# Retention's value blocks moved ahead of its queries and keys, two of them as one block of 1024 columns with four seven-product units

## The chip, the cores and the metric

The kernel runs on one core of a Trainium2 chip. Its engines have instruction queues of their own, which run in order and wait for each other by semaphores: TensorE (PE in the profile; PEld is its loading of weights), VectorE (DVE), ScalarE (ACT), GpSimd (POOL) and SyncE (SP), which here only issues the DMAs. The metric is the device time of one execution in microseconds: before the change 2271.42 us, the median of three runs (2270.95 to 2271.64).

## What is computed

A decoder layer for 256 tokens of width 2048 in float32: a half FFN, two token mixers side by side (retention and sliding-window attention), a second half FFN, and a gated input embedding, each followed by a layer norm. Of this the change touches the first projections of the mixers:

```python
rq, rk, rv, rg, aq, ak, av, gate_r, gate_a = jnp.split(h @ w_in[i], SPLIT_POINTS, axis=-1)
rq = rotary(rq.reshape(B, S, RET_HEADS, RET_DK), positions, RET_DK, RET_THETA)
rk = rotary(rk.reshape(B, S, RET_HEADS, RET_DK), positions, RET_DK, RET_THETA) * (RET_DK ** -0.5)
rv = rv.reshape(B, S, RET_HEADS, RET_DV)
ro = head_group_norm(retention_chunkwise(rq, rk, rv), ret_gn_g[i]).astype(h.dtype)
```

`rq` and `rk` have 1024 columns each, `rv` has 2048: four blocks of 512.

## The kernel before

**Numbers in two halves.** Every matrix product is made of three matmuls: each operand is split into a high half (a cast by ScalarE, L98, tiles `h...`) and a low half (a subtraction by VectorE, L99, tiles `l...`), and low x high, high x high and high x low are summed in a PSUM bank (L374, L375, L376; for queries and keys L325 and L333). A weight chunk is 512 KB, 128 x 1024 values. One of values, `w_rv`, holds two k-tiles of 128 rows for 512 columns; with two halves of 128 tokens it costs TensorE 2 x 2 x 3 = 12 matmuls of 512 columns, ScalarE one cast and VectorE one subtraction.

**Sevens.** Where two column blocks of 512 are made together, two chunks (one of each column block, the same two k-tiles) form a 2 x 2 problem: two k-tiles by two column blocks, against two token halves by two k-tiles. A *plain* pair, `P`, is two `Single` chunks and takes 24 matmuls. A `Seven`, `S`, does the same with seven products instead of eight, 21 matmuls, at the price of sums: VectorE makes four sums of weights of 512 columns (L170 to L173, tiles `u`, `v`) and four low halves instead of two (of the first chunk, of a quarter `b`, of `u` and of `v`): eight operations. The tokens need sums too, *forms* (`forms_of`, `whole`, `seven_forms`): for each group of four k-tiles one addition of 1024 columns (L457), four of 256 (L445 to L448), a cast and a low half. At the end `seven_common` folds the banks of the four products p1, p6, p7 and q5 (bank names ending in `s0` to `s3`) with one copy and four VectorE operations (L479 to L483), and four more add the plain banks (`a0`, `a1`, `b0`, `b1`). The third to the sixth product of a seven use forms. A block with sevens holds all eight PSUM banks.

**The order of the work.** The order is written out by hand (`manual_schedule`). A planner (`plan`, `fill`, `take`, `done`) loads chunks and prepares them in the order of the plan as far ahead as places allow (`slots_for_weights`: so many of 46 places in SBUF, each of 4 KB per partition). After each chunk `run_side` also runs a step of `lazy`: first of all `sums_ahead`, which prepares sevens of the second FFN ahead of time (two operations L238 and L239, two L242 and L243, low halves L248 and L250) and stores them to DRAM, and a rotary table for the attention.

**This stage.** After the first FFN, `norm.first` does the rest of the layer norm while TensorE makes the first block of values, `rv0`, as its tokens become ready. `values` then splits the block's two banks (tiles `rvh`, `rvl`). Then come eight groups of queries and keys (`rqk`, 16 matmuls of 512 and 16 of 256 columns per two chunks, each group followed by a rotation, L1064 to L1075), then blocks 1, 2 and 3 of values (`tokens_out`, 96 matmuls each), then the gates of retention, during which the heads' scores run as side jobs with the decay tables (`dec`, asked for by ScalarE's queue). Both stages have 14 places for weights. Later in the mixers, two gate blocks `ga0` and `ga1` are already blocks of 1024 columns with four sevens each (`GATE_UNITS`, `mixer_block`), with 22 places.

Of the kernel before, what the change touches and what calls it, by code (L numbers as in the profile page):

```python
# [8 lines left out]
F32 = mybir.dt.float32  # L9
# [46 lines left out]
def layer(ctx: ExitStack, tc: tile.TileContext, io):  # L56
# [13 lines left out]
    def banks(name):  # L70
        return [bank(name + str(j)) for j in range(2)]

    def slot(shape, dt, name):
        return slots.tile(shape, dt, tag="slot", name=name)
# [22 lines left out]
    def split(dst_hi, dst_lo, src, lo_engine=None):  # L97
        act.copy(dst_hi, src)  # L98
        (lo_engine or dve).tensor_tensor(dst_lo, src, dst_hi, ALU.subtract)  # L99
# [119 lines left out]
    def sums_ahead(items, wait, every):  # L219


        def pause():
            for _ in range(every):
                yield

        pairs = [[Chunk(k) for k in items[0]]]
        for _ in range(wait):
            yield
        for j, (key, _) in enumerate(items):
            a, b = pairs.pop()  # L230
            b11, b21, b12, b22 = a.of(a.raw, 0), a.of(a.raw, 1), b.of(b.raw, 0), b.of(b.raw, 1)
            u, v = (slot([P, 2, 512], F32, w + a.name) for w in "uv")
            t1, t3, t2, t4 = (x.rearrange("p (g n) -> p g n", g=2) for x in (u[:, 0], u[:, 1], v[:, 0], v[:, 1]))
            parts = [slot([P, 2, 512], F32R, w + a.name) for w in ("hu", "lu", "hv", "lv")]
            uh, ul, vh, vl = parts
            away = [dram.tile([P, 2, 512], F32, name=f"{w}{a.name}") for w in ("hud", "lud", "hvd", "lvd")]
            put_by_sums[key] = away
            dve.tensor_tensor(t1, b11, b12, ALU.add)  # L238
            dve.tensor_tensor(t3, b12, b22, ALU.add)  # L239
            yield from pause()  # L240
            act.copy(uh, u)
            dve.tensor_tensor(t2, b11, t3, ALU.add)  # L242
            dve.tensor_tensor(t4, t2, b21, ALU.add)  # L243
            yield from pause()
            act.copy(vh, v)
            if j + 1 < len(items):
                pairs.append([Chunk(k) for k in items[j + 1]])
            dve.tensor_tensor(ul, u, uh, ALU.subtract)  # L248
            yield from pause()
            dve.tensor_tensor(vl, v, vh, ALU.subtract)  # L250
            for e in range(2):
                sync.dma_start(away[e], parts[e].bitcast(F32))
            yield from pause()
            for e in range(2, 4):
                sync.dma_start(away[e], parts[e].bitcast(F32))
# [44 lines left out]
    def slots_for_weights(n, ahead=45, far=90):  # L300
        room.update(slots=n, ahead=ahead, far=far)
# [84 lines left out]
    def tokens_out(key, n_k, lhs, ps, n=512, before=None):  # L386

        nk = 1024 // n
        sums = [Sum(ps[t][:, :n], n_k) for t in range(2)]
        for c in range(n_k // nk):  # L390
            u = take(key + (c,))
            tokens_chunk(u.chunk, c * nk, lhs, sums, (0, 1), range(nk))
            done(u)
            run_side()
# [9 lines left out]
    def block(name, units, keys, lhs, forms, sums, fold, before=None):  # L404


        sevens = [p for kind, p in units if kind != "P"]
        if sevens:
            p1, p6, p7, q5 = (Sum(bank(f"{name}s{j}"), len(sevens)) for j in range(4))
        for j, (kind, p) in enumerate(units):  # L410
            if before is not None:
                before(j)
            if kind == "P":
                for n in range(2):
                    u = take(keys(n, p))
                    tokens_chunk(u.chunk, 2 * p, lhs, [sums[t][n] for t in range(2)], (0, 1))
                    done(u)
                    run_side()
                continue
            u = take(keys(0, p))  # L420
            a11, a12 = (half_of(lhs(2 * p + e), 0) for e in range(2))
            a22 = half_of(lhs(2 * p + 1), 1)
            f5, f6, f7, f3 = forms(p)
            q2, q3, q4 = sums[0][0], sums[0][1], sums[1][0]
            steps = [
                (p1, a11, u.b11), (q2, a12, u.b21), (q3, f3, u.b22), (q5, f5, u.t1),
                (p7, f7, u.t3), (p6, f6, u.t2), (q4, a22, u.t4),
            ]
            if p == sevens[-1]:
                steps = [steps[j] for j in (0, 3, 5, 4, 1, 2, 6)]  # L430
            for to, left, right in steps:
                to.add(left, right)
            done(u)
            run_side()
            if p == sevens[-1]:
                fold(p1.ap, p6.ap, p7.ap, q5.ap)
# [27 lines left out]
    def units_of(order, sevens, ahead=()):  # L464

        sevens, ahead = list(sevens), list(ahead)
        plain = [p for p in range(KD // 2) if p not in sevens + ahead]
        of = {"S": sevens, "D": ahead, "P": plain}
        return [(kind, of[kind].pop(0)) for kind in order]

    def block_sums(ps, units, n_k):

        s = sum(kind == "S" for kind, p in units)
        return [[Sum(ps[t][n], n_k - (2 * s if t and n else s)) for n in range(2)] for t in range(2)]
# [16 lines left out]
    def plan_tokens(key, n_k, nk=2):  # L491
        for c in range(n_k // nk):
            plan.append(Single(key + (c,)))
# [585 lines left out]

    GATE_UNITS = units_of("PPSSPSSP", (0, 1, 2, 3))  # L1080
    RET_UNITS = units_of("PPPSPSPP", (0, 1))
    gate_keys = lambda b: lambda n, p: ("w_in_f2", 29 + 4 * b + 2 * n, p)
    ret_keys = lambda b: lambda n, p: ("w_ret2", 4 * b + 2 * n, p)

    def plan_mixers():
        plan_tokens(("w_rv", 0), KD)
        for grp in range(8):
            plan_features([("w_in_f", grp)], KD)
        for blk in range(1, 4):
            plan_tokens(("w_rv", blk), KD)  # L1090
        for grp in range(8, 16, 2):
            plan_tokens(("w_in_f2", grp), KD)
        plan_tokens(("w_av",), KD, nk=4)
        for grp in (20, 16, 17, 18, 19):
            plan_features([("w_in_f", grp)], KD)
        for grp in range(21, 29, 2):
            plan_tokens(("w_in_f2", grp), KD)
        for b in range(2):
            block_units(GATE_UNITS, gate_keys(b))
        for j in range(0, 8, 2):  # L1100
            plan_tokens(("w_att2", j), KD // 2)
        for b in range(2):
            block_units(RET_UNITS, ret_keys(b))
        for blk in range(4):
            plan_tokens(("w_mix", blk), KD)
# [7 lines left out]
    def mixers(ht, norm, residual, keepers, away):  # L1113
        cos_r, sin_r = trig["r"]
        rhs = lambda k: (ht[:, k, :S], ht[:, k, S:])
        both_halves = lambda k: ht[:, k, :]
        rq = [slot([P, 4, S], F32, f"rq{j}") for j in range(2)]
        rk = [slot([P, 4, S], F32, f"rk{j}") for j in range(2)]

        def rotated(grp, ps):  # L1120
            who = (rq, rk)[grp // 4][grp % 4 // 2]
            rotate(ps, f"rr{grp}", who[:, grp % 2 * 2 : grp % 2 * 2 + 2, :], cos_r, sin_r, SH_R)

        rv = []

        def values(blk, ps):
            hi, lo = (slot([P, 2, 512], F32R, f"rv{w}{blk}") for w in "hl")
            for t in range(2):
                split(hi[:, t], lo[:, t], ps[t])
            rv.append((hi, lo))  # L1130

        ps = banks("rv0")
# [7 lines left out]
            tokens_chunk(u.chunk, 2 * c, rhs, [sums[t][0] for t in range(2)], (0, 1))  # L1140
            done(u)
        values(0, ps)
        slots_for_weights(14)
        ahead = [(gu_keys("f2", j)(0, p), gu_keys("f2", j)(1, p)) for j in AHEAD for p in AHEAD[j]]
        lazy.append(sums_ahead(ahead[:2], 3, 2))
        lazy.append(rotary_table("a"))
        lazy.append(sums_ahead(ahead[2:5], 2, 2))
        lazy.append(sums_ahead(ahead[5:8], 2, 3))
        for grp in range(8):
            ps = banks(f"rqk{grp}")  # L1150
            features_out([(("w_in_f", grp), ps)], KD, both_halves)
            rotated(grp, ps)
        grp = 8
        decay = [slot([P, 2, 384], F32, f"dec{j}") for j in range(4)]
        for j in range(4):
            act.dma_start(decay[j], io["decay"][:, 2 * j : 2 * j + 2, :])
        for blk in range(1, 4):
            ps = banks(f"rv{blk}")
            tokens_out(("w_rv", blk), KD, rhs, ps)
            values(blk, ps)  # L1160

        ret_t = [None] * HR
        gate_v = [None] * HR
        keep = {}
# [223 lines left out]
        for grp in (18, 19):  # L1388
            attention_features(grp)

        made = {}
        forms = lambda p: made[p // 2](p % 2)
        slots_for_weights(18)
        sig = []
        for j in range(4):
# [8 lines left out]
            for t in range(2):  # L1404
                act.copy(sig[-1][:, t], ps[t])
        assert not side

        def mixer_block(name, units, keys, lhs):

            ps = [banks(name + w) for w in "ab"]  # L1410
            got = []
            block(name, units, keys, lhs, forms, block_sums(ps, units, KD), lambda *a: got.extend(seven_common(*a)))
            for n in range(2):
                for t in range(2):
                    dve.tensor_tensor(got[n][:, t], got[n][:, t], ps[t][n], ALU.add)
            return got

        slots_for_weights(22)
        for b in range(2):
# [375 lines left out]
```

## Time and profile before

| what | value |
|---|---|
| median of three runs | 2271.42 us |
| span of the profiled execution | 2269.2 us |
| TensorE's granted clock, mean | 0.999 |
| DMA | 515.72 MB, mean 227 GB/s |
| casts and low halves of the values' chunks (`hw_rv`, `lw_rv`) | 32 each, 1.05 and 1.22 us |
| last matmul of block 0 of values, first of the queries | 732.5 us, 732.7 us |
| blocks 1 to 3 of values | 822 to 887 us |

The profile is one execution, taken by the hardware profiler; times inside it count from its first instruction. Matmuls overlap, so their listed lengths (390 ns for 512 columns) are longer than the distance from one to the next. A row of the timeline gives start, length, engine, line, operation, tiles out and in with their shapes, a count, and the idle time of the engine before it with what ended it.

### The profile page before, as it was taken

Reading aid. Unit: us, or ns where it says so; the run is one execution under the profiler, and the core shown is the slowest. Engines: PE = TensorE matmul, PEld = TensorE weight load, DVE = VectorE, ACT = ScalarE, POOL = GpSimd, SP = SyncE. Lnnn points to the kernel's source line nnn. Section 1 sums busy time; section 2 is a strip of 40 time slices with the busy share of each in tenths; the row PEclk is TensorE's granted clock in tenths of the full one; section 3 lists DMA queues with packets and bytes.
Section 4 is the critical chain, followed back from the end, with each engine's and each line's share of the span. In section 5 each row is a group of like instructions: output and inputs, shape, how many; then the busy total and the mean of one; then the engine's idle time right before and its main releaser. Section 6 shows DMA issues by size and latency. Waiting matters only on the chain.

```text
span 2269.2 us, 29180 instructions
## 1 busy us (share of the span) xinstructions
PE 2262.1 (100%) x10497; PEld 1880.1 (83%) x10497; DVE 1996.8 (88%) x2586; ACT 1224.6 (54%) x1493; POOL 2.3 (0%) x9
## 2 busy tenths in 40 slices
PE   9999999999999999999999999999999999999998
PEld 8888888888888888888778888888888888888887
DVE  7999999999989887888789788689999999889887
ACT  6555555556555444445566554455555565555543
POOL 0000000000000000000000000000000000000000
PEclk9999999999999999999999999999999999999999
DMA  8666665665587878765446668787867766555872
GB/s 301 206 202 195 197 212 177 205 205 187 211 287 258 293 284 295 255 227 190 145 154 219 194 203 294 278 287 241 299 242 250 257 197 218 197 189 210 290 268 75
DMA packets 211130, 515.72 MB, mean 227 GB/s; under 512 B 16413, under 2 KB 20893, under 8 KB 210985
## 3 DMA queue, kind: packets, MB, share of 16 engines
q1 hardware_dynamic: 209000, 511.28, 66.4%
q10 hardware_dynamic: 1984, 2.58, 0.4%
q8 instruction: 82, 1.34, 0.2%
q14 instruction: 64, 0.52, 0.1%
HBM read 484.43 MB, written 29.36 MB: 226 GB/s over the span
## 4 chain that ended last, share of the span: by engine, by line
PE 99%; DVE 0%; ACT 0%; issue 0%; ACTq 0%; POOL 0%; POOLq 0%
PE f1g L376 3%; PE f1g L374 3%; PE f1g L375 3%; PE f2g L376 3%; PE f2g L374 3%; PE f2g L375 3%; PE rqk L325 3%; PE f1u L376 2%; PE f1u L374 2%; PE f1u L375 2%; PE f2u L374 2%; PE f2u L376 2%; PE f2u L375 2%; PE aqk L325 2%; PE f2d L374 2%; PE f1d L375 2%
## 5 line engine op out<-in xcount | busy, mean ns | idle before, releaser
L99 DVE TENSOR_TENSOR lf_gu<-rf_gu,hf_gu 128x1024 fp32r<-128x1024 f32 (+1 forms) x274 | 323.3, 1211 | 13.1 <-ACT hf_gu L98 12.2
L98 ACT CAST hf_gu<-rf_gu 128x1024 fp32r<-128x1024 f32 (+1 forms) x274 | 274.1, 1043 | 29.9 <-DMA rf_gu<-in_f_gu 29.6
L99 DVE TENSOR_TENSOR lf_down<-rf_down,hf_down 128x1024 fp32r<-128x1024 f32 x150 | 178.8, 1220 | 17.4 <-ACT hf_down L98 15.3
L99 DVE TENSOR_TENSOR lw_in_f<-rw_in_f,hw_in_f 128x1024 fp32r<-128x1024 f32 x140 | 167.5, 1219 | 24.9 <-ACT hw_in_f L98 24.7
L98 ACT CAST hf_down<-rf_down 128x1024 fp32r<-128x1024 f32 x150 | 151.8, 1050 | 48.8 <-DMA rf_down<-in_f_down 22.3
L98 ACT CAST huf_gu<-uf_gu 128x1024 fp32r<-128x1024 f32 x70 | 73.8, 1054 | 146.6 <-DVE uf_gu L171 135.1
L98 ACT CAST hw_in_f<-rw_in_f 128x1024 fp32r<-128x1024 f32 x140 | 140.3, 1050 | 3.0 <-PE rv L375 1.4
L374 PE MATMUL f1g<-hf_gu,xt 128*128 128x512 f32 x247 | 96.5, 391 | 0.0
L376 PE MATMUL f1g<-lf_gu,xt 128*128 128x512 f32 x247 | 96.4, 390 | 0.0
L375 PE MATMUL f1g<-hf_gu,xt 128*128 128x512 f32 x247 | 96.1, 389 | 0.0
L98 ACT CAST hvf_gu<-vf_gu 128x1024 fp32r<-128x1024 f32 x70 | 73.8, 1054 | 29.9 <-DVE vf_gu L173 29.2
L971 ACT ACTIVATE eve<-eve 128x1024 f32<-128x1024 f32 x20 | 21.2, 1062 | 126.1 <-DVE eve L970 126.1
L99 DVE TENSOR_TENSOR luf_gu<-uf_gu,huf_gu 128x1024 fp32r<-128x1024 f32 x70 | 85.3, 1219 | 0.0
L99 DVE TENSOR_TENSOR lvf_gu<-vf_gu,hvf_gu 128x1024 fp32r<-128x1024 f32 x70 | 85.3, 1218 | 0.0
L374 PE MATMUL f2g<-hf_gu,ht 128*128 128x512 f32 x217 | 84.6, 390 | 0.0
L376 PE MATMUL f2g<-lf_gu,ht 128*128 128x512 f32 x217 | 84.5, 390 | 0.0
L375 PE MATMUL f2g<-hf_gu,ht 128*128 128x512 f32 x217 | 84.4, 389 | 0.0
L374 PE MATMUL f1u<-hf_gu,xt 128*128 128x512 f32 x212 | 83.4, 393 | 0.0
L376 PE MATMUL f1u<-lf_gu,xt 128*128 128x512 f32 x212 | 82.5, 389 | 0.0
L375 PE MATMUL f1u<-hf_gu,xt 128*128 128x512 f32 x212 | 82.5, 389 | 0.0
L374 PE MATMUL f2u<-hf_gu,ht 128*128 128x512 f32 x172 | 68.2, 397 | 0.0
L376 PE MATMUL f2u<-lf_gu,ht 128*128 128x512 f32 x172 | 66.9, 389 | 0.0
(1465 smaller groups left out, 6558.1 us busy)
## 6 DMA issues: line engine op xcount, KB each, us to landing
rf_gu<-in_f_gu SPq DMA_DIRECT2D x360, 512.0 KB
rf_down<-in_f_down SPq DMA_DIRECT2D x176, 512.0 KB
rw_in_f<-in_w_in_f SPq DMA_DIRECT2D x148, 512.0 KB
rw_rv<-in_w_rv SPq DMA_DIRECT2D x32, 512.0 KB
rw_ret<-in_w_ret SPq DMA_DIRECT2D x32, 512.0 KB
rw_mix<-in_w_mix SPq DMA_DIRECT2D x32, 512.0 KB
rw_pg<-in_w_pg SPq DMA_DIRECT2D x32, 512.0 KB
rw_att<-in_w_att SPq DMA_DIRECT2D x16, 512.0 KB
```

What stands on the lines that cost most here:

```text
L98: act.copy(dst_hi, src)
L99: (lo_engine or dve).tensor_tensor(dst_lo, src, dst_hi, ALU.subtract)
L325: pe.matmul(ps[f], hi[:, kk, f * P : (f + 1) * P], rhs(k), start=k == 0, stop=k == n_k - 1,)
L374: pe.matmul(o, al, bh, start=first, stop=False)
L375: pe.matmul(o, ah, bh, start=False, stop=False)
L376: pe.matmul(o, ah, bl, start=False, stop=self.left == 0)
L971: act.activation(g, g, AF.Silu)
```

## The change

It does four things. The plan and the code put all values ahead of the queries and keys. Blocks 1 and 2 are made together as one block of 1024 columns by `mixer_block` (moved up, unchanged), with the units plain 4, seven 0, plain 5, seven 1, plain 6, seven 2, plain 7, seven 3; its token forms for two groups are made right after block 0, and `values` splits each folded result of 1024 columns at once. These blocks run with the 24 places that `norm.first` is followed by, and 14 places are set only before block 3. The tiles for queries and keys (four places) are taken only after block 3.

```diff
+    VALUE_UNITS = units_of("PSPSPSPS", (0, 1, 2, 3))
+    value_keys = lambda n, p: ("w_rv", 1 + n, p)
...
         plan_tokens(("w_rv", 0), KD)
+        block_units(VALUE_UNITS, value_keys)
+        plan_tokens(("w_rv", 3), KD)
         for grp in range(8):
             plan_features([("w_in_f", grp)], KD)
-        for blk in range(1, 4):
-            plan_tokens(("w_rv", blk), KD)
...
-        rq = [slot([P, 4, S], F32, f"rq{j}") for j in range(2)]
-        rk = [slot([P, 4, S], F32, f"rk{j}") for j in range(2)]
+        rq, rk = [None] * 2, [None] * 2
...
         def values(blk, ps):
             hi, lo = (slot([P, 2, 512], F32R, f"rv{w}{blk}") for w in "hl")
-            for t in range(2):
-                split(hi[:, t], lo[:, t], ps[t])
+            if isinstance(ps, list):
+                for t in range(2):
+                    split(hi[:, t], lo[:, t], ps[t])
+            else:
+                split(hi, lo, ps)
             rv.append((hi, lo))
...
         values(0, ps)
-        slots_for_weights(14)
+        for g in range(2):
+            made[g] = forms_of([ht[:, 4 * g : 4 * g + 4, :]], f"rvf{g}")
...
         lazy.append(sums_ahead(ahead[5:8], 2, 3))
+        for n, v in enumerate(mixer_block("rvs", VALUE_UNITS, value_keys, rhs)):
+            values(1 + n, v)
+        made.clear()
+        slots_for_weights(14)
+        ps = banks("rv3")
+        tokens_out(("w_rv", 3), KD, rhs, ps)
+        values(3, ps)
+        rq[:] = [slot([P, 4, S], F32, f"rq{j}") for j in range(2)]
+        rk[:] = [slot([P, 4, S], F32, f"rk{j}") for j in range(2)]
         for grp in range(8):
             ps = banks(f"rqk{grp}")
             features_out([(("w_in_f", grp), ps)], KD, both_halves)
...
             act.dma_start(decay[j], io["decay"][:, 2 * j : 2 * j + 2, :])
-        for blk in range(1, 4):
-            ps = banks(f"rv{blk}")
-            tokens_out(("w_rv", blk), KD, rhs, ps)
-            values(blk, ps)
```

More of the change, by code (lines that the diff above doesn't have):

```diff
@@ L1124, in mixers, with mixer_block @@
         rv = []
+        made = {}
+        forms = lambda p: made[p // 2](p % 2)
+        def mixer_block(name, units, keys, lhs):
+            ps = [banks(name + w) for w in "ab"]
+            got = []
+            block(name, units, keys, lhs, forms, block_sums(ps, units, KD), lambda *a: got.extend(seven_common(*a)))
+            for n in range(2):
+                for t in range(2):
+                    dve.tensor_tensor(got[n][:, t], got[n][:, t], ps[t][n], ALU.add)
+            return got
         def values(blk, ps):
             hi, lo = (slot([P, 2, 512], F32R, f"rv{w}{blk}") for w in "hl")
-            for t in range(2):
-                split(hi[:, t], lo[:, t], ps[t])
+            if isinstance(ps, list):
+                for t in range(2):
+                    split(hi[:, t], lo[:, t], ps[t])
+            else:
+                split(hi, lo, ps)
             rv.append((hi, lo))
@@ L1389, in mixers @@
             attention_features(grp)
-        made = {}
-        forms = lambda p: made[p // 2](p % 2)
         slots_for_weights(18)
@@ L1406, in mixers @@
         assert not side
[L1408 to L1416, printed above, removed]
         slots_for_weights(22)
```

## The prediction

> **What bounds the kernel now.** I read first the page's busy times, then TensorE's own waits.
>
> ```profile
> span 2269.2 us, 29180 instructions
> PE 2262.1 (100%) x10497; PEld 1880.1 (83%) x10497; DVE 1996.8 (88%) x2586; ACT 1224.6 (54%) x1493; POOL 2.3 (0%) x9
> ...
> PE warm L1674 <- POOL ident masks.py:199: 1.4, 1, 1.4
> PE pln L1568 <- DVE plnst L1566: 0.2, 1, 0.2
> PE plnt L1559 <- DVE plnm L1554: 0.2, 1, 0.2
> ```
>
> TensorE waits 1.8 us in 2269, so a matmul fewer is a matmul's time saved, and nothing else can be gained. VectorE is the second engine. Three stretches of the windows view show where it has room; the columns are the stretch, its length, then busy time of PE, PEld, DVE, ACT and POOL, TensorE's granted clock, DMA share and GB/s.
>
> ```profile
> 730.00:742.00 12.00, 12.00 (x66) 10.37 (x65) 9.98 (x11) 7.09 (x9) 0.00 (x0) 1.00 1.02 399
> 844.00:866.00 22.00, 22.00 (x99) 18.22 (x98) 15.65 (x17) 11.12 (x13) 0.00 (x0) 1.00 0.90 302
> 1200.00:1240.00 40.00, 40.00 (x178) 33.14 (x177) 39.42 (x48) 22.01 (x24) 0.00 (x0) 1.00 0.61 199
> ```
>
> The second is a plain block of values, with VectorE idle 6.3 of 22 us. The third is a gate block with four sevens: VectorE is busy 39.4 of 40 us, and TensorE holds only because the weights for the block were prepared during an easier stage before it. The change puts such a block right behind the norm (first row), where no easier stage lies ahead. So I follow VectorE's queue there by hand.
>
> **The gain.** Matmuls of 512 columns follow each other at one pace: 21 of them from the first row to the second.
>
> ```profile
> 727.98 0.23 PE rv L374
> ...
> 732.74 1.36 PE rqk L325 x6
> ```
>
> (732.74 - 727.98) / 21 = 0.2267 us. Two plain pairs of chunks cost 24 matmuls, a seven 21; four sevens save 12 x 0.2267 = 2.72 us. The order in which the built program issues its matmuls has 12 fewer, and no other kind is added.
>
> **What VectorE gets to do, and when.** These rows of its timeline give each price as the distance from one start to a later one, so that overlap is not counted twice. The columns are start, length, line, operation, tiles, count, and idle time before with its releaser.
>
> ```profile
> 728.41 6.89 DVE L99 TENSOR_TENSOR lw_in_f<-rw_in_f,hw_in_f 128x1024 fp32r<-128x1024 f32 x6
> 735.22 1.28 DVE L99 TENSOR_TENSOR rvl<-rv,rvh 128x512 fp32r<-128x512 f32 x2
> 736.42 2.35 DVE L99 TENSOR_TENSOR lw_in_f<-rw_in_f,hw_in_f 128x1024 fp32r<-128x1024 f32 x2
> ...
> 744.11 0.76 DVE L1065 TENSOR_TENSOR rr0v<-rqk,rr0lo 128x256 f32<-128x256 f32 x2 [4.13 <-ACT rr0lo L1064]
> ...
> 747.63 2.35 DVE L99 TENSOR_TENSOR lw_in_f<-rw_in_f,hw_in_f 128x1024 fp32r<-128x1024 f32 x2
> ...
> 828.09 0.69 DVE L238 TENSOR_TENSOR uf_gu<-rf_gu,rf_gu 128x512 f32<-128x512 f32 x1
> ...
> 829.30 2.35 DVE L99 TENSOR_TENSOR lw_rv<-rw_rv,hw_rv 128x1024 fp32r<-128x1024 f32 x2
> 831.57 0.69 DVE L242 TENSOR_TENSOR vf_gu<-rf_gu,uf_gu 128x512 f32<-128x512 f32 x1
> ...
> 832.90 2.35 DVE L99 TENSOR_TENSOR lw_rv<-rw_rv,hw_rv 128x1024 fp32r<-128x1024 f32 x2
> 835.17 1.22 DVE L248 TENSOR_TENSOR luf_gu<-uf_gu,huf_gu 128x1024 fp32r<-128x1024 f32 x1
> ...
> 1142.32 1.22 DVE L457 TENSOR_TENSOR gaf1w<-ht 128x1024 f32<-128x1024 f32 x1
> ...
> 1146.29 1.23 DVE L99 TENSOR_TENSOR gaf1l<-sums,gaf1h 128x1024 fp32r<-128x1024 f32 x1 [1.17 <-ACT gaf1h L98]
> 1147.44 1.22 DVE L99 TENSOR_TENSOR lw_in_f<-rw_in_f,hw_in_f 128x1024 fp32r<-128x1024 f32 x1
> ...
> 1169.47 0.69 DVE L170 TENSOR_TENSOR uw_in_f<-rw_in_f,rw_in_f 128x512 f32<-128x512 f32 x1
> ...
> 1176.14 0.68 DVE L170 TENSOR_TENSOR uw_in_f<-rw_in_f,rw_in_f 128x512 f32<-128x512 f32 x1
> 1203.20 0.69 DVE L480 TENSOR_TENSOR evw<-eve,ga0s 128x512 f32<-128x512 f32 x1
> ```
>
> A chunk's low half costs 6.81 / 6 = 1.14 us; block 0's two low halves 1.20; a seven's eight operations 1176.14 - 1169.47 = 6.67; one set of forms of the tokens 1147.44 - 1142.32 = 5.12, with 1.17 us of standing still for ScalarE in it; the first two sums prepared ahead for the second FFN 1.21, the next two 1.33, their low half 1.14; the first fold operation (L480) 0.69.
>
> Before, VectorE had eight chunks' low halves to make from 728.41 and then stood idle 4.13 us. In the changed program its queue from 728.41 on runs, in the order in which it is issued (my sums): two low halves of the plain pair 4, to 730.7; seven 0, 737.4; pair 5, 739.6; block 0's rvl, 740.8; forms 0, **746.0**; forms 1, 751.1; seven 1, 757.7; half of pair 6, two sums ahead, the other half, 761.2; seven 2, 767.9; two sums ahead, pair 7, one low half ahead, 772.7; seven 3, 779.3; four low halves of block 3's chunks with one low half ahead among them, 785.0; two sums ahead, 786.2; L480, **786.9**. That is 58.5 us of queue without a pause.
>
> **TensorE beside it.** It leaves block 0 at 732.74 as before.
> 1. Pair 4 takes 24 matmuls, to 738.2; the first two products of seven 0 need no forms, 6 more, to 739.5. The third multiplies the low half of form 0, ready at 746.0: it stands **6.5 us** (A). Seven 0 and pair 5 go on to 754.9.
> 2. Sevens 1 and 2 and pairs 6 and 7 just hold: seven 1's first low half is there at 751.1 + 6.67 - 0.60 - 2 x 1.14 = 754.9 (three low halves of it follow) and is needed by its third matmul at 755.3. Seven 3 does not: TensorE is there at 775.4; the low halves that its first three products need come at 776.5, 778.2 and 779.3, each later than the matmul before them allows, **some 2 us** (B).
> 3. Block 3's second bank is the one that product p6 leaves, and L480 reads that. TensorE has the rest of seven 3 and three matmuls into the first bank done near 783 and waits until 786.9, **some 4 us** (C).
>
> A shorter way to the same sum, which needs none of the middle: without a wait the 180 matmuls of the block and three of block 3 end at 732.74 + 183 x 0.2267 = 774.2. L480 ends at 786.9. Loss 12.7, gain 2.72: **10.0 us net**.
>
> After C, TensorE reaches chunk 4 of block 3 45 matmuls later, at 797.1; VectorE needs seven fold operations and block 1 and 2's rvl (7 x 0.65 + 2 x 1.14) and that chunk's low half, 794.9. From there VectorE leads again, with four chunks in hand at the queries; the groups of queries load it as they did.
>
> **TensorE's clock.** A wait of this length is nowhere inside the old kernel; only its ends show one.
>
> ```profile
> 2262.95 0.96 PE L1568 MATMUL pln<-lnrow,plnst 66*128 66x512 f32 x3 [0.21 <-DVE plnst L1566]
> ...
> 2262.00:2263.00 1.00, 0.79 (x4) 0.36 (x4) 0.86 (x3) 0.26 (x1) 0.00 (x0) 1.00 0.00 0
> ...
> 2264.00:2265.00 1.00, 0.00 (x0) 0.00 (x0) 0.59 (x1) 0.75 (x2) 0.00 (x0) 1.00 0.59 204
> 2265.00:2266.00 1.00, 0.00 (x0) 0.00 (x0) 0.00 (x0) 0.00 (x0) 0.00 (x0) 0.72 0.92 339
> 2266.00:2267.00 1.00, 0.00 (x0) 0.00 (x0) 0.00 (x0) 0.00 (x0) 0.00 (x0) 0.50 1.02 385
> ...
> L1674 PE MATMUL warm<-ident x19: 421/421/473, 1.4 to 5.3; 128*128 128x128 f32 x19
> ...
> L623 PE MATMUL lnps<-ident,f1y x32: 270/272/275, 701.6 to 724.3; 128*128 128x128 f32 x32
> ```
>
> The granted clock falls to a half about 1.5 us after the last matmul ends (2263.9), and the transposes of the start, which come from rest, take 421 ns against 272 for the same form later, for the whole 3.9 us from 1.4 to 5.3. If a wait does this here, some 3.9 us run at half pace: 1.95 us lost. After A it costs nothing more, because B and C end with VectorE's queue and swallow it. After C nothing follows that would: between 0 and 2.0. I take 1.3, nearer to the upper end, since C is 4 us long and the row falls after 1.5, but TensorE was already idle a fifth of the time before that (second row).
>
> [...]
>
> **Sum.** The profiled execution's span is 2269.2; the runs' median is 2271.42, 2.2 more, which lies around the span. 2271.4 + 10.0 + 1.3 = **2282.7 us**.
>
> **What is costed at nothing.** Weight loads: a pair of chunks fetched for seven 1 takes the places in the queue where two chunks for queries stood, and those were split at 736.42 without a DMA wait; seven 1 needs them at 751. The decay tables are now asked for right behind the queries and used in the first gate chunks.
>
> ```profile
> 822.16 0.33 ACTq L1156 DMA_DIRECT2D dec<-in_decay  x1
> ...
> 825.49 1.31 SPq L112 DMA_DIRECT2D rw_rv<-in_w_rv  x2
> ...
> SPq L112 <- DMA dec<-in_decay: 10.3, 3, 9.2
> ```
>
> The weight queue was released by the first table's landing at 825.5, 3.3 us after its issue; VectorE wants it after the last group's rotation (747.63 - 744.11 = 3.5) and one low half, 4.6 us after. Queued behind that wait are the low halves from the gates' sixth chunk on, needed 5 x 12 x 0.2267 = 13.6 us after the gates begin, and the scores of head 0, which TensorE wants after the third chunk, 8.2 us. A table that lands more than some 2 us late would cost; the price is 0 to 3 us.
>
> **Rivals.**
> - Not slower (4%): VectorE has the forms ready by 739.5, TensorE never waits, all 2.7 us stay: 2268.7. The gate block speaks for it, where the same work did not hold TensorE; against it, there the second set of forms was ready at 1147.4, some 15 us before the block began (its fold stands at 1203.2, 180 x 0.2267 = 40.8 after its start), and here both stand behind 12.4 us of queue. It decides at one point, whether forms 0 end before 739.5.
> - Forms alone (15%): A is paid, the rest is made up because sums ahead and block 3's halves get out of the way or the bank comes free sooner: 6.5 - 2.7 + 0 to 2 for the clock, 2275.2 to 2277.2.
> - More waits (11%): the decay tables or chunks fetched late add up to 3 us, or the clock stays low longer: 2285 to 2288.
> - Forecast (70%): 2281.4 to 2283.4.
>
> That the edit does not do what it says is out: 12 matmuls are gone from the program.
>
> **The numbers.** What this kernel can tell from no change is about 0.2%, 4.5 us: 2266.9 to 2276.0. All of the first rival and about two thirds of the second fall within; faster by more would need a gain which no row offers. Faster 0.02, same 0.14, slower 0.84. Range 2275 to 2287.
>
> **What would show it.** Right: 128x512 rv matmuls 12 fewer; TensorE idle 6 to 7 us with VectorE's low half of the forms as releaser; a second wait of about 4 us at block 3's second bank, released by L480; granted clock below 1 near both; TensorE's first query matmul near 809, gates some 10 us later than before. Wrong: no wait at the forms (first rival), no second wait (second rival), or a wait on the decay tables.

## The result and the profile after

| | before | after |
|---|---|---|
| median of the runs, side by side | 2271.53 us (2270.95 to 2271.95) | 2284.05 us (2283.23 to 2284.63) |
| span of the profiled execution | 2269.2 us | 2282.8 us |
| TensorE's granted clock, mean | 0.999 | 0.996 |

The ratio is 1.0055, 95% interval 1.0043 to 1.0067: the changed kernel is 0.55% slower. The gain is there all the same. The head of the page and its busy times (the last number in each part is the count of instructions) show 10485 matmuls where there were 10497:

```profile
span 2282.8 us, 29225 instructions
...
PE 2265.0 (99%) x10485; PEld 1881.8 (82%) x10485; DVE 2025.6 (89%) x2628; ACT 1233.5 (54%) x1502; POOL 2.3 (0%) x9
```

TensorE's waits (total, times, longest) now begin with two lines that were not there before, ahead of the one of the kernel's start:

```profile
PE rvsa L374 <- DVE rvf0l L99: 6.5, 1, 6.5
PE rv L374 <- DVE evw L480: 3.3, 1, 3.3
PE warm L1683 <- POOL ident masks.py:199: 1.4, 1, 1.4
```

The first is the wait for the forms (A in the prediction), the second the one for block 3's second bank (C). There is none at the last seven's low halves (B) and none on the decay tables. VectorE's timeline shows what TensorE waited for:

```profile
740.98 1.22 DVE L457 TENSOR_TENSOR rvf0w<-ht 128x1024 f32<-128x1024 f32 x1
...
744.90 1.23 DVE L99 TENSOR_TENSOR rvf0l<-sums,rvf0h 128x1024 fp32r<-128x1024 f32 x1 [1.11 <-ACT rvf0h L98]
...
779.52 1.22 DVE L99 TENSOR_TENSOR lw_rv<-rw_rv,hw_rv 128x1024 fp32r<-128x1024 f32 x1
780.65 1.22 DVE L250 TENSOR_TENSOR lvf_gu<-vf_gu,hvf_gu 128x1024 fp32r<-128x1024 f32 x1
781.79 3.49 DVE L99 TENSOR_TENSOR lw_rv<-rw_rv,hw_rv 128x1024 fp32r<-128x1024 f32 x3
785.19 0.69 DVE L238 TENSOR_TENSOR uf_gu<-rf_gu,rf_gu 128x512 f32<-128x512 f32 x1
785.79 0.69 DVE L239 TENSOR_TENSOR uf_gu<-rf_gu 128x512 f32<-128x512 f32 x1
786.39 0.68 DVE L480 TENSOR_TENSOR evw<-eve,rvss 128x512 f32<-128x512 f32 x1
```

The forms end at 744.90 + 1.23 = 746.13. The last seven's last low half is done by 779.52; then four low halves of block 3's chunks (the first of them is the row at 779.52) and three operations for the second FFN stand ahead of L480, which ends at 787.07. TensorE's timeline around both waits:

```profile
739.31 0.39 PE L376 MATMUL rvsa<-lw_rv,ht 128*128 128x512 f32 x1
746.18 0.80 PE L374 MATMUL rvsa<-bw_rv,rvf0l 128*128 128x512 f32 x1 [6.48 <-DVE rvf0l L99]
...
752.37 0.39 PE L374 MATMUL rvsa<-hw_rv,ht 128*128 128x512 f32 x1
...
783.42 0.39 PE L376 MATMUL rv<-lw_rv,ht 128*128 128x512 f32 x1
787.13 0.79 PE L374 MATMUL rv<-hw_rv,ht 128*128 128x512 f32 x1 [3.32 <-DVE evw L480]
...
793.32 0.40 PE L374 MATMUL rv<-hw_rv,ht 128*128 128x512 f32 x1
```

From 746.18 to 752.37 and from 787.13 to 793.32 lie 15 matmuls each: 6.19 us where 15 x 0.2267 = 3.40 are due. So each wait is followed by 2.79 us lost, nearly all of it at half clock: the first matmul takes 0.6 us, the twelve after it some 0.43 each, and the last two are back at nearly the full pace. The windows view has the clock in its third number from the end:

```profile
741.00:742.00 1.00, 0.00 (x0) 0.00 (x0) 1.00 (x2) 0.00 (x0) 0.00 (x0) 0.83 0.83 188
751.00:752.00 1.00, 1.00 (x4) 0.77 (x3) 1.00 (x3) 0.46 (x1) 0.00 (x0) 0.55 0.00 0
...
786.00:787.00 1.00, 0.00 (x0) 0.00 (x0) 1.00 (x2) 0.00 (x0) 0.00 (x0) 0.52 1.05 315
792.00:793.00 1.00, 1.00 (x4) 0.80 (x3) 1.00 (x2) 1.00 (x2) 0.00 (x0) 0.57 0.67 274
```

The account of the stage: 6.64 (739.31 to 746.18, less one matmul) + 2.79 + 3.48 (783.42 to 787.13, less one matmul) + 2.79 - 2.72 saved = 12.98 us. The first row of the retention gates, before and then after, says the same (the two numbers in us are the first and the last start in what is shown):

```profile
L374 PE MATMUL rg<-hw_in_f,ht x56: 389/389/478, 887.2 to 929.2; 128*128 128x512 f32 x56
```

```profile
L374 PE MATMUL rg<-hw_in_f,ht x39: 388/390/475, 900.4 to 929.8; 128*128 128x512 f32 x39
```

They start 13.2 us later, and the span is 13.6 longer: nothing comes back later, and next to nothing is added. (The profiled execution is the slowest of its four, at 2284.63 us; the medians lie 12.5 apart.)

### The profile page after: what moved, and what is told of

It is laid out like the page before. It is cut to its first block, busy times and chain, and to the rows that moved or that the text cites. A ratio compares the mean times of both kernels' runs of the same rounds, so it can differ in the third digit from the quotient of the medians.

```text
span 2282.8 us, 29225 instructions
## 1 busy us (share of the span) xinstructions
PE 2265.0 (99%) x10485; PEld 1881.8 (82%) x10485; DVE 2025.6 (89%) x2628; ACT 1233.5 (54%) x1502; POOL 2.3 (0%) x9
## 4 chain that ended last, share of the span: by engine, by line
PE 97%; DVE 1%; DMA 1%; ACT 0%; issue 0%; ACTq 0%; SPq 0%; DVEq 0%
PE f1g L374 3%; PE f1g L376 3%; PE f1g L375 3%; PE f2g L376 3%; PE f2g L375 3%; PE f2g L374 3%; PE rqk L325 3%; PE f1u L374 2%; PE f1u L375 2%; PE f1u L376 2%; PE f2u L375 2%; PE f2u L376 2%; PE f2u L374 2%; PE aqk L325 2%; PE f2d L374 2%; PE f1d L376 2%
## 5 line engine op out<-in xcount | busy, mean ns | idle before, releaser
L99 DVE TENSOR_TENSOR lf_gu<-rf_gu,hf_gu 128x1024 fp32r<-128x1024 f32 (+1 forms) x274 | 323.2, 1211 | 13.9 <-ACT hf_gu L98 12.8
```

## The experiments

Two theories stood against each other. By the first, the end of VectorE's whole queue, L480, sets the time, and it doesn't matter where on the way TensorE stands. By the second, the wait for the forms is the loss, and all the rest is made up. A third question was what the half clock costs. Times are medians, and each ratio is against the kernel before run beside it, which was at 2271.1 to 2271.3; the changed kernel's 2284.05 is from the set in which before was at 2271.5. So a difference of some 0.4 us to the changed kernel says nothing by itself; where it matters, the start of the gates' first matmul in the trace is given too (900.41 in the changed kernel).

### The move without the sevens

```diff
-        for g in range(2):
-            made[g] = forms_of([ht[:, 4 * g : 4 * g + 4, :]], f"rvf{g}")
...
-        for n, v in enumerate(mixer_block("rvs", VALUE_UNITS, value_keys, rhs)):
-            values(1 + n, v)
+        for blk in range(1, 4):
+            ps = banks(f"rv{blk}")
+            tokens_out(("w_rv", blk), KD, rhs, ps)
+            values(blk, ps)
```

> All four blocks of values ahead of the queries and keys, none of them with sevens, no forms, 24 places for blocks 1 to 3. Theory (the sevens' work behind the norm is the cause): VectorE has 12 low halves of 1.14 us per 21.8 us of TensorE and keeps ahead, no wait: 2271.0 to 2272.5. Rival (the move costs by itself, by the places, the decay tables or the order of loads): 2275 or more.

Measured: 2271.11 us, ratio 1.0000 (0.9991 to 1.0009). TensorE has no wait in this stage. The move costs nothing, neither by its places nor by the decay tables; all of the loss belongs to the sevens and their forms. (A block has eight chunks, so VectorE has eight low halves per 21.8 us and not the twelve of the expectation: more room still.)

### The plain pairs first

```diff
-    VALUE_UNITS = units_of("PSPSPSPS", (0, 1, 2, 3))
+    VALUE_UNITS = units_of("PPPPSSSS", (0, 1, 2, 3))
```

> The four plain pairs of the block come first, the four sevens after them; everything else is as in the changed kernel. Theory (VectorE's queue as a whole sets the end): the forms are ready some 740 us in and wanted at about 756, so the wait of 6.5 us at them goes; but VectorE has the same operations ahead of L480, which still ends near 787, and the waits appear at the sevens and at block 3's second bank instead. Time 2281.3 to 2284.1, where the lower end is for a clock loss of 2.7 us that does not come back. Rival (the wait at the forms is the loss): without it and its half clock 2284.05 - 6.5 - 2.7 = 2274.9.

Measured: 2281.7 us, ratio 1.0044 (1.0029 to 1.0060). TensorE's waits of this kernel, and then two operations of its VectorE timeline:

```profile
PE rvss L376 <- DVE lw_rv L99: 6.7, 3, 2.8
PE rv L374 <- DVE evw L480: 2.5, 1, 2.5
...
PE rvss L376 <- DVE luw_rv L99: 0.8, 1, 0.8
```

```profile
740.67 1.22 DVE L99 TENSOR_TENSOR rvf0l<-sums,rvf0h 128x1024 fp32r<-128x1024 f32 x1 [1.12 <-ACT rvf0h L98]
...
786.49 0.68 DVE L480 TENSOR_TENSOR evw<-eve,rvss 128x512 f32<-128x512 f32 x1
```

The forms are ready at 741.9, long before they are wanted, and their wait is gone. Three waits at the sevens' low halves stand in its place (6.7 us, each at the next seven), and L480 starts at 786.49, 0.1 us from where it was. The second theory asked for 2274.9 and falls. The gates start at 899.42, 1.0 us sooner than in the changed kernel. That much is half clock saved: behind the bank it lasts here only from 788.70 to 792.12 (granted clock 0.85 in the window from 788 and 0.94 in that from 792). The medians lie 2.4 us apart; for the rest of that no cause is shown.

### The sums for the second FFN later

```diff
-        lazy.append(sums_ahead(ahead[:2], 3, 2))
-        lazy.append(rotary_table("a"))
-        lazy.append(sums_ahead(ahead[2:5], 2, 2))
-        lazy.append(sums_ahead(ahead[5:8], 2, 3))
...
         values(3, ps)
+        lazy.append(sums_ahead(ahead[:2], 3, 2))
+        lazy.append(rotary_table("a"))
+        lazy.append(sums_ahead(ahead[2:5], 2, 2))
+        lazy.append(sums_ahead(ahead[5:8], 2, 3))
```

> The sums prepared ahead for the second FFN begin only after block 3 of values. Theory (queue): 6.0 us fewer ahead of L480 (1.21 + 1.33 + 1.2 for three pairs of sums, two low halves of 1.14), so it ends near 781, before TensorE wants the bank at 783.4; the wait at the forms stays at 6.5 us, the wait of 3.3 us at the bank and the 2.7 us of half clock behind it go: 2278.0, up to 2280 if the sums find less room later. Rival (the forms alone count, or the bank waits for something else): 2284.

Measured: 2280.39 us, ratio 1.0040 (1.0026 to 1.0054), span 2278.5. An operation of its VectorE timeline, its waits on TensorE, and the first row of the gates:

```profile
780.46 0.69 DVE L480 TENSOR_TENSOR evw<-eve,rvss 128x512 f32<-128x512 f32 x1
```

```profile
PE rvsa L374 <- DVE rvf0l L99: 6.5, 1, 6.5
...
PE at L1373 <- DVE asc L1363: 1.2, 2, 0.8
```

```profile
L374 PE MATMUL rg<-hw_in_f,ht x47: 389/389/476, 894.0 to 929.4; 128*128 128x512 f32 x47
```

L480 starts 5.9 us sooner, as the sum of what was taken away (6.0) said. The wait at the bank and its half clock are gone (the granted clock is 1.00 in every window from 752 to 797), and the gates start 6.4 us sooner than in the changed kernel. The span is only 4.3 us shorter: some of it is lost again behind the gates, where new waits of 1.2 us in the attention are the only ones that the profile names. The time lies 0.4 us above the expected range.

### The fold's first step sooner

```diff
             for to, left, right in steps:
                 to.add(left, right)
+            begun = ()
+            if name == "rvs" and p == sevens[-1]:
+                begun = (seven_begin(p1.ap, p6.ap),)
             done(u)
             run_side()
             if p == sevens[-1]:
-                fold(p1.ap, p6.ap, p7.ap, q5.ap)
+                fold(p1.ap, p6.ap, p7.ap, q5.ap, *begun)
```

`seven_begin` holds the first lines of `seven_common`, L478 to L480, in which the rest then goes on.

> The changed kernel with one thing moved: the copy and the operation that free the bank of p6 are issued right behind the last seven, ahead of the sums and of block 3's four low halves instead of behind them. No operation is added or taken away. Theory (the second wait is a place in VectorE's queue): the operation ends near 781, when p6 is complete, ahead of TensorE's need at 783.4; the wait of 3.3 us and the half clock behind it go, 2284.05 - 3.3 - 2.7 = 2278.0, between 2277.5 and 2279.5. Rival (what is moved back, block 3's low halves, is then late instead): 2281 to 2284.

Measured: 2278.8 us, ratio 1.0034 (1.0021 to 1.0046). Its VectorE timeline (the freeing operation is L483 here) and TensorE's first matmul into the freed bank:

```profile
781.89 1.22 DVE L99 TENSOR_TENSOR lw_rv<-rw_rv,hw_rv 128x1024 fp32r<-128x1024 f32 x1
783.02 0.68 DVE L483 TENSOR_TENSOR evw<-eve,rvss 128x512 f32<-128x512 f32 x1
```

```profile
783.76 0.50 PE L374 MATMUL rv<-hw_rv,ht 128*128 128x512 f32 x1
```

With not one operation fewer, 5.3 us of the 12.5 are back, and the time lies in the expected range. The operation came 2 us later than expected, since two low halves and one for the FFN had been issued ahead of the last seven's end, but still in time: the matmul follows the one before it by 0.46 us. So C was a place in the queue. What the rival had in mind is there too, but small: a wait of 0.4 us at one of the low halves that were moved back.

What is left, 7.5 us above the kernel before, is for the most part A. TensorE stands from 739.42 to 746.28 (6.63 us, less one matmul), and the ten matmuls from 746.28 to 750.55 lose 2.0 us, most of it to the half clock; less the 2.72 saved, that makes 5.9. With C gone, no later wait of that size swallows these terms. That is read from the trace; no run fills A with the fold put early.

### Filling the waits with work

Matmuls whose result is overwritten keep TensorE busy while it would wait. At the forms, 27 of them:

```diff
             for to, left, right in steps:
+                if name == "rvs" and p == 0 and to is q3:
+                    for _ in range(27):
+                        pe.matmul(p7.ap, a11[0], u.b11[0], start=True, stop=True)
                 to.add(left, right)
```

> 27 matmuls of 512 columns more (6.1 us at 0.2267) run where TensorE waits for the forms, into a bank that its first product overwrites; the result is the same. Theory (VectorE's queue sets the end, what the clock costs after the first wait is swallowed): the clock stays full there, waits of some 2 us appear at the last seven in its place, the wait at block 3's second bank still ends near 787: time 2283.5 to 2284.5, no change. Rival (the half clock is a loss of its own): 2284.05 - 2.7 = 2281.3.

Measured: 2283.61 us, ratio 1.0055 (1.0041 to 1.0069), as the changed kernel. A window behind the forms (clock, third from the end) and TensorE's waits:

```profile
746.00:752.00 6.00, 5.71 (x25) 4.71 (x26) 4.75 (x9) 2.52 (x3) 0.00 (x0) 1.00 0.10 23
```

```profile
PE rv L374 <- DVE evw L483: 3.5, 1, 3.5
...
PE rvss L376 <- DVE luw_rv L99: 0.8, 1, 0.8
PE rvss L376 <- DVE lw_rv L99: 0.4, 1, 0.4
PE rvsa L374 <- DVE rvf0l L99: 0.4, 1, 0.4
...
PE rvss L376 <- DVE lvw_rv L99: 0.2, 1, 0.2
```

The clock is full at 746 to 752, and the waits at the last seven's low halves (0.4 + 0.8 + 0.2) appear, which the changed kernel did not show: there TensorE, 2.79 us later behind its half clock, came late enough. The time does not move, and the gates start at 900.64.

At block 3's bank, 14 of them:

```diff
         ps = banks("rv3")
+        first = ready[0].chunk.columns(0)[0]
+        for _ in range(14):
+            pe.matmul(ps[0], rhs(0)[0][:, :P], first, start=True, stop=True)
         tokens_out(("w_rv", 3), KD, rhs, ps)
```

> 14 matmuls of 512 columns more (3.2 us) run ahead of block 3 of values into its first bank, which its first product overwrites, so that TensorE works while it would wait for the second bank; the result is the same. Theory (the half clock behind this wait is a loss of its own, as nothing follows that would swallow it): the clock stays full from 787 to 793 and the time falls by 2.7 us, 2284.05 - 2.7 = 2281.3. Rival (VectorE's queue swallows it too): no change, 2284.

Measured: 2281.54 us, ratio 1.0046 (1.0032 to 1.0059): 2.5 us back by the medians, and the gates start 2.4 us sooner, at 897.97. The window behind the wait now has a full clock:

```profile
787.00:793.00 6.00, 5.66 (x25) 4.66 (x26) 5.86 (x10) 2.23 (x3) 0.00 (x0) 1.00 0.94 383
```

Both fillings together:

> Both fillings together: 27 matmuls at the forms and 26 ahead of block 3 of values; the result is the same. Theory (only the clock after the second wait counts): as with the second filling alone, 2281.3. Rival (each half clock costs its 2.7 us): 2278.6.

Measured: 2283.22 us, ratio 1.0053 (1.0039 to 1.0067), neither of the two. The 26 matmuls ran to 788.2, later than the bank came free, so the filling itself cost time; the run does not tell the theories apart. With 17 in place of 26:

> Both fillings again, with 17 matmuls in place of 26 ahead of block 3: in the run with 26 they lasted from 782.3 to 788.2, past the point where L480 had freed the bank (786.7), so it could not answer. 17 end at 786.2. Theory (the half clock after the forms is swallowed by VectorE's queue, the one behind the bank is a loss of its own): as with the filling ahead of block 3 alone, 2281.5. Rival (each costs its 2.7 us): 2278.8.

Measured: 2281.54 us, ratio 1.0046 (1.0031 to 1.0061), the same as with the filling at the bank alone (the gates start at 897.61). So, as long as the bank comes free at 787, the half clock behind the forms costs nothing of its own, and the one behind the bank costs some 2.5 us.

### The four sevens where the blocks stood before

The kernel before, with blocks 1 and 2 as one block of four sevens behind the queries and keys:

```diff
+            if grp in (4, 6):
+                g = grp // 2 - 2
+                made[g] = forms_of([ht[:, 4 * g : 4 * g + 4, :]], f"rvf{g}")
+            if grp == 7:
+                slots_for_weights(20)
             features_out([(("w_in_f", grp), ps)], KD, both_halves)
...
-        for blk in range(1, 4):
-            ps = banks(f"rv{blk}")
-            tokens_out(("w_rv", blk), KD, rhs, ps)
-            values(blk, ps)
+        for n, v in enumerate(mixer_block("rvs", VALUE_UNITS, value_keys, rhs)):
+            values(1 + n, v)
```

> The same block with four sevens, but where blocks 1 and 2 stood before the change, behind the queries and keys; its forms are made during the queries' groups 4 and 6, it has 20 places, and the decay tables are asked for behind it. Theory (VectorE's work for a block must fit beside TensorE's): four sevens add 4 x 4.39 = 17.6 us to blocks 1 and 2, where VectorE was idle 6.3 of 22 us, 11.7 in 41; 5.9 us too many, less 2.7 gained: 2271.2 + 3.2 = 2274.4, up to 2277 with a half clock. Rival (only the place right behind the norm is wrong): everything fits, 2268.5.

Measured: 2283.17 us, ratio 1.0051 (1.0039 to 1.0064). The rival is far off, but so is the number of the theory: the time lies 6 us above its upper end and 8.8 above the sum. Three windows of this kernel (PE, PEld, DVE, ACT, POOL), two of its waits, and a window of the kernel before:

```profile
812.00:822.00 10.00, 9.48 (x53) 8.30 (x54) 9.85 (x16) 6.17 (x9) 0.00 (x0) 1.00 0.50 171
...
830.00:840.00 10.00, 7.88 (x33) 5.83 (x34) 9.89 (x15) 3.71 (x6) 0.00 (x0) 1.00 0.58 210
...
870.00:878.00 8.00, 4.55 (x15) 3.04 (x14) 7.84 (x11) 1.53 (x2) 0.00 (x0) 0.77 1.03 401
```

```profile
PE rv L374 <- DVE evw L480: 2.7, 1, 2.7
PE rvsa L376 <- DVE lw_rv L99: 1.5, 1, 1.5
```

```profile
777.00:822.00 45.00, 45.00 (x259) 39.57 (x258) 39.87 (x66) 18.65 (x27) 0.00 (x0) 1.00 0.79 272
```

VectorE is busy almost without a gap from 812 on. My sum had put the forms into the queries' groups at no cost, but VectorE had only 5.1 us free there in 45, and two sets take 10.2; and it had left out the four low halves of block 3 that stand ahead of L480 here too (4 x 1.14). Together that is 5.1 + 4.6 = 9.7 us, near what was missing; that these two make it up is worked out, not tested. So neither of the two places tried has room for four sevens, and the one right behind the norm is not special.

### Two sevens

```diff
-    VALUE_UNITS = units_of("PSPSPSPS", (0, 1, 2, 3))
+    VALUE_UNITS = units_of("PPPPPPSS", (0, 1))
...
-        for g in range(2):
+        for g in range(1):
             made[g] = forms_of([ht[:, 4 * g : 4 * g + 4, :]], f"rvf{g}")
```

> The changed kernel with two sevens in place of four (chunk pairs 0 and 1 only, behind six plain pairs) and one set of forms. Theory (queue): L480's end falls by 2 x 4.39 + 5.1 = 13.9 us, from 786.9 to 773.0, and TensorE wants it behind 186 matmuls, 732.74 + 42.2 = 774.9: no wait; 6 matmuls less, 1.4 us: 2271.2 - 1.4 = 2269.8. Rival (two sevens in a row at the end wait anyway, with a half clock behind): 2272 to 2275.

Measured: 2269.66 us (2268.94 to 2270.14), ratio 0.9994 (0.9985 to 1.0003). Its VectorE timeline and all of TensorE's waits:

```profile
773.32 0.68 DVE L480 TENSOR_TENSOR evw<-eve,rvss 128x512 f32<-128x512 f32 x1
```

```profile
PE warm L1683 <- POOL ident masks.py:199: 1.4, 1, 1.4
PE pln L1577 <- DVE plnst L1575: 0.2, 1, 0.2
PE plnt L1568 <- DVE plnm L1563: 0.2, 1, 0.2
```

L480 ends at 774.0, where the ledger of prices said 773.0, and no wait is left. It is 14.4 us faster than the changed kernel, and the order alone does not do that: with four sevens put last the waits stayed. Against the kernel before, the 1.5 us of the medians agree with the six matmuls saved (1.4), but the interval takes in no change.

## Why the prediction was right, point by point

The median, 2284.05 us, lies within the range and 1.4 us above the sum of 2282.7. It also lies above the forecast's own 2281.4 to 2283.4 and below the rival "more waits": the mechanism held, and one term, the clock, was too small.

- **Gain, 2.72 us: right.** 12 matmuls fewer; the medians of the kernel with two sevens and no wait agree with half of it.
- **VectorE's queue: right to 0.2 us.** The forms were forecast to end at 746.0 and ended at 746.1; L480 at 786.9 and 787.1. The runs show that this end, not the place of any one wait, sets the time: without the wait for the forms L480 did not move and the time fell by 2.4 us at most; with 5.9 us less in the queue, or L480 earlier in it, the second wait went. Two sevens bring the same ledger under TensorE's own time, and nothing is lost.
- **A, 6.5 us: right.**
- **B, some 2 us: not there as waits.** TensorE came to the last seven at 778.21, where I had 775.4, because the half clock after A had cost it 2.79 us. When the clock was kept up, B appeared with 1.4 us. Since both end with the same queue, the sum did not feel it.
- **C, some 4 us: 3.3**, and 3.5 with A filled. The last matmul ahead of it started at 783.42, where I had TensorE done near 783. The sum does not feel this either.
- **The half clock after A swallowed: right, as long as C stands.** Filling A changed nothing, with C open or filled. With the fold's first step put sooner, C is gone, and by the trace A's half clock is paid; no run tests that alone.
- **The half clock after C: the term that was mis-sized.** I took 1.3 us out of 0 to 2.0, and even the upper end was too low. The trace has 2.79 and the filling got 2.5 back. I had the price from the transposes at the start of the kernel, 421 ns against 272 for 3.9 us. That this was a half clock was my estimate: the windows view gives the granted clock there as 1.00. After both waits here the half clock lasted 5.7 us of work (the last section has the lengths in other traces). With 2.8 in place of 1.3, the sum is 10.0 + 2.8 = 12.8, against 13.0 by the account above, 12.5 by the medians and 13.6 by the spans.
- **Costed at nothing: right.** No wait on weights or decay tables; the move alone costs nothing.
- **The signs:** the first matmul of queries came at 811.0, not near 809, and the gates 13.2 us later, not some 10. Both follow from the clock term. The 93 matmuls of block 3 that follow C end at 786.9 + 93 x 0.2267 = 808.0 without it, 809.3 with my 1.3 and 810.8 with 2.8; from the 10 us of the gates I had left it out.
- **Rivals:** "forms alone" falls with the plain pairs put first; "not slower" falls with A itself; of "more waits", the clock that stays low longer did happen, after C.

## What to carry to other kernels

Where one engine trades its work for another's, write out the other engine's queue from the last point at which it has a lead to the first of its operations that frees something, and compare its end with the first engine's own time: that difference is the loss, however the waits are spread. Moving a wait gains next to nothing as long as that end stands, and filling one gains nothing but the half clock behind the last of them (2.5 us here); taking operations out of the queue, or putting the freeing operation earlier in it, gains more. In these traces a half clock went with the waits on TensorE of 2.5 to 6.5 us (granted clock 0.50), and none with those of 2.3 us and less that stood alone (1.00 from 757 to 771 with the plain pairs first); what it costs counts only where no later wait for the same queue swallows it.

## What the runs showed of the hardware

The half clock did not end a fixed time after the work came back, though in the changed kernel it was 5.7 us both times. From the windows of 1 us, reading 0.5 as half and the mixed ones as shares, it lasted from 741.66 to 751.90 and from 786.04 to 792.86 in the changed kernel: 10.24 and 6.82 us. Two more windows show a shorter one, in the kernel with the plain pairs first:

```profile
778.00:779.00 1.00, 0.38 (x1) 0.38 (x2) 1.00 (x2) 1.00 (x2) 0.00 (x0) 0.73 0.94 336
781.00:782.00 1.00, 1.00 (x4) 0.81 (x3) 1.00 (x2) 0.04 (x1) 0.00 (x0) 0.56 1.00 401
```

From 778.46 to 781.88: 3.42 us. The two above are three times and twice that, within 0.02 us; what sets these lengths is not shown.

When the clock falls and comes back differs from one kernel's trace to the next, though the work is the same up to then. The kernel with the fold's first step sooner has the same wait A (6.5 us), with the work back at 746.28, but another half clock:

```profile
743.00:744.00 1.00, 0.00 (x0) 0.00 (x0) 0.85 (x3) 0.08 (x1) 0.00 (x0) 0.77 0.25 102
750.00:751.00 1.00, 1.00 (x5) 0.80 (x4) 0.87 (x1) 1.00 (x3) 0.00 (x0) 0.82 0.00 0
```

It lasts from 743.54 to 750.36, 6.82 us, of which 4.1 us are work, where the changed kernel had 10.24 us and 5.7 of work (746.18 to 751.90; after C 787.13 to 792.86). With the sums later and with the bank filled, it was 5.4 and 4.2 us of work behind the same wait: from 744.82 to 751.64 (granted clock 0.91 in the window from 744 and 0.68 in that from 751) and from 743.78 to 750.62 (0.89 from 743 and 0.69 from 750). In the kernel with the plain pairs first the work behind the bank was back at 787.23 and the clock fell only at 788.70: 3.42 us of half clock, all of it work. What a wait cost thus hung on when the clock fell and came back, which the trace of before could not tell. Only one execution of each kernel was profiled, so none shows what sets these times, or how far they differ between executions of one kernel.
